# Rotary queries with fewer copies, input loads moved ahead, paged queries loaded early, and low halves moved to VectorE in a hybrid decoder layer

## The chip, the cores and the metric

The kernel runs on one core of a Trainium2 chip. The metric is the device time of one execution in microseconds (us). The core's engines each work through an instruction stream of their own, in order: TensorE (PE, matmuls and transposes; its weight loads are shown apart as PEld), VectorE (DVE), ScalarE (ACT), GpSimd (POOL) and SyncE (SP, which issues most DMAs). An instruction that waits holds up everything behind it on its engine.

## The reference

One inference step of a layer with two branches over the same input x: 1024 prompt tokens and 8 x 8 sampled tokens (1088 in all), width 1024. Cut to what matters here:

```python
xn = rmsnorm(x, w["norm_in"])
z = xn @ w["w_in"]
u_s, g_s, cq, ckv_raw, kr_raw, g_a, m_s, m_a = split_in(z)
y_s, h_last = s5_branch(u_s, ssm_h0, w)      # y = scan + d * u; zg = gelu(y)
                                             # out = zg * sigmoid(zg @ w_glu + b_glu)
y_s = (y_s * silu(g_s)) @ w["w_br_ssm"]
cq = rmsnorm(cq, w["mla_q_norm"])
q = einsum('blr,rhd->blhd', cq, w["mla_w_uq"])                 # 16 heads, 64 + 32
q_rope = apply_rope(q[..., 64:], cos, sin)   # x1, x2 = halves of 16:
                                             # [x1*cos - x2*sin, x1*sin + x2*cos]
...
o_lat = attend(q_lat, q_rope, ckv, k_rope)   # prompt: causal softmax;
                                             # sampled: 4096 paged tokens each, and themselves
y_a = (o * silu(g_a)) @ w["w_br_attn"]
merged = sigmoid(m_s) * y_s + sigmoid(m_a) * y_a
h = x + merged @ w["w_out"]                  # then rmsnorm(h, norm_final)
```

Everything is float32, and the new latents, rotary keys and scan states are outputs too.

## The kernel before

Each large product is computed from split operands. A float32 tensor is cast to a shorter format (the high half, `whi`, `z` by ScalarE in most places), the difference is taken as the low half (`wlo`, on VectorE or GpSimd), and three matmuls (high by high, high by low, low by high) add up in PSUM (`mm3`, L154). Activations stand transposed: eight rows of 128 channels by 1088 tokens, as `xT`, `z`, `aT`, `oT`, with a high and a low tile for each row. A product runs over chunks of 368, 368 and 352 tokens.

Streams of work are woven by generators that yield estimated costs, with an offset of priority for each stream. A scheduler with a timeline model then fixes the order on every engine, so the order of the code is only a hint. `behind` adds a dependency that this scheduler sees; it makes no semaphore wait.

The stages in the order of time: the norm and transposes of x and the scan input u, with the scan's setup (`s5_setup`) beside it, up to about 115 us; the scan with gate products as filling; latents; rotary queries and keys (484 to 541 us); query, key and value projections, with the gather of cached rotary keys, to 668; prompt attention with gate products and the gelu (`gy`, `gw`) to 975; then the gated unit on z, the ssm branch on a, and paged attention, to 1565; the attention branch on o; and the output product from 1682.

Places that the change touches:

- Input loads (L209): x is loaded in three groups of three tiles into six buffers, and each group's load is issued when its turn comes. The scan's setup loads c (L394, L395), b (L399, L400), d (L499) and the state (L505) on the same queue, SP.
- Rotary queries (L881 to L890): for each of 4 x 3 chunks, ScalarE copies the product out of PSUM, then copies it again in four blocks of 32 partitions, with the halves exchanged, into `qrot`. GpSimd multiplies the one by the cosines and the other by the sines, VectorE adds them, and the sum is split and stored to `qr_dram`.
- `load_split` (L109 to L112): loads a row of z, a or o over the place of an earlier tensor's row, casts it on ScalarE and takes the low half; GpSimd does so for rows 1, 3 and 5, VectorE for the others. The row of z stands where the row of `xT` stood, so its load waits for the last matmul on that row.
- The paged attention's queries `qs` (L1109, twelve loads), its mask (L1101) and its own new keys (L1114 to L1121) are set up when the paged attention begins. Its tiles are placed as they come.
- The final norm's weights `gf` are loaded at the start of the attention branch.

## Time and profile before

| | |
|---|---|
| Time, three runs | 1794.87, 1798.14, 1799.96 us; median 1798.14 |
| The profiled execution | 1795.67 us, of which the span is 1793.9 us |
| Mean granted clock of TensorE | 0.983 of full speed |
| Busy in the span | PE 96%, PEld 91%, DVE 61%, ACT 53%, POOL 37% |
| The chain that ended last, by engine | PE 73%, DMA 8%, DVE 6%, ACT 5%, issue 3%, POOL 3% |

TensorE is busy nearly all the time, so what other engines do counts only where TensorE waits for them. A row of a timeline gives the start, the busy time, engine, line, operation, output<-input and shapes, and in brackets the idle time just ahead of it with what ended that. The granted clock is a share of full speed; 0.50 is the lower of its two levels. Runs of the same form are joined in one row with a count (x3).

### The profile page before, as it was taken

The numbers are of one execution on the slowest core, as the hardware profiler recorded it, in microseconds if no ns is written. First come the engines' busy times: TensorE is split into PE (matmuls) and PEld (weight loads), VectorE is DVE, ScalarE is ACT, GpSimd is POOL, SyncE is SP. The second block draws the span as 40 slices with busy tenths as digits, with TensorE's granted clock in tenths as the row PEclk, the third lists the DMA queues.
The fourth block names the chain that finished last, engine by engine and source line by source line (L and its number), as shares of the span: only waits on it lengthen the run. The fifth ranks groups of instructions, "written<-read, shape, count | busy, mean of one in ns | idle before, by whom it ended". The sixth has DMA issues, their size and how long they took to land.

```text
span 1793.9 us, 32266 instructions
## 1 busy us (share of the span) xinstructions
PE 1715.3 (96%) x11434; PEld 1628.7 (91%) x11434; DVE 1102.7 (61%) x2552; ACT 944.5 (53%) x2287; POOL 671.6 (37%) x694
## 2 busy tenths in 40 slices
PE   6999999989989999999997999989999999999997
PEld 6999999989989998999996999879989999999997
DVE  6758898233354435878876887586656766554322
ACT  5236657623373434777765665266656666432222
POOL 1000000023462214656654555665545555232223
PEclk9999999999999999999998999999999999999999
DMA  8465345453559997667656453665555555375602
GB/s 214 110 150 151 110 127 132 121 148 110 154 167 308 321 321 204 151 163 187 172 142 202 128 149 86 213 222 173 182 173 165 184 176 181 103 238 162 180 1 100
DMA packets 263194, 299.59 MB, mean 167 GB/s; under 512 B 40273, under 2 KB 223289, under 8 KB 256761
## 3 DMA queue, kind: packets, MB, share of 16 engines
q1 hardware_dynamic: 252856, 240.89, 46.9%
q0 software_dynamic: 7872, 48.24, 8.0%
q10 hardware_dynamic: 2304, 8.39, 1.2%
q8 instruction: 91, 1.49, 0.3%
q14 instruction: 71, 0.57, 0.1%
HBM read 201.79 MB, written 95.66 MB: 166 GB/s over the span
## 4 chain that ended last, share of the span: by engine, by line
PE 73%; DMA 8%; DVE 6%; ACT 5%; issue 3%; POOL 3%; SPq 2%; POOLq 0%; ACTq 0%; DVEq 0%
PE mm L154 36%; PE sc L154 5%; PE acc L1155 5%; PE sc L1009 4%; PE tr L154 3%; PE tr L1045 3%; PE sc L1129 2%; PE sc L1218 2%; PE acc L1058 2%; PE acc L1059 2%; PE tr L1129 1%; PE tr L1218 1%; DMA ck<-cache_ckv,pidx 1%; DMA v_dram<-vt 1%; DMA kr_dram<-dks 1%
## 5 line engine op out<-in xcount | busy, mean ns | idle before, releaser
L154 PE MATMUL mm<-xT,whi 128*128 128x368 f32 (+1 forms) x1920 | 505.6, 337 | 3.3 <-ACT xT L237 1.5
L154 PEld LDWEIGHTS mm<-xT,whi 128*128 128x128 f32 x1920 | 342.1, 191 | 7.5 <-ACT xT L237 2.1
L154 PE MATMUL mm<-xT,wlo 128*128 128x368 f32 (+1 forms) x960 | 319.6, 334 | 0.0
L102 POOL TENSOR_TENSOR cl<-ck,ch 128x1024 fp32r<-128x1024 f32 x64 | 157.8, 2467 | 168.0 <-ACT ch L96 149.0
L154 PEld LDWEIGHTS mm<-xT,wlo 128*128 128x128 f32 x960 | 182.7, 190 | 1.0 <-issue 0.2
L102 DVE TENSOR_TENSOR pTl<-tr,pTh 128x256 fp32r<-128x256 f32 (+1 forms) x248 | 126.0, 511 | 39.6 <-ACT pTh L96 22.8
L96 ACT CAST pTh<-tr 128x256 fp32r<-128x256 f32 (+1 forms) x248 | 110.5, 449 | 73.3 <-PE tr L1045 58.0
L1009 PE MATMUL sc<-K,Q 128*128 128x384 f32 (+5 forms) x576 | 132.9, 349 | 8.9 <-ACT p L1021 8.9
L1191 POOL DMA_INDIRECT dkr<-cache_krope,pidx x32 | 34.1, 1067 | 267.0 <-DMA rt<-k_rope_tok 259.7
L1026 POOL TENSOR_SCALAR p<-p,sm 128x128 f32<-128x128 f32 (+7 forms) x128 | 97.4, 766 | 87.2 <-DVE sm L1025 41.6
L1021 ACT ACTIVATE p<-sc,sm 128x128 f32<-128x128 f32 (+2 forms) x192 | 110.8, 583 | 25.2 <-DVE sm L1016 14.9
L1045 PE MATMUL tr<-ident,p 128*128 128x128 f32 x576 | 113.0, 276 | 6.0 <-DVE sm L1016 3.0
L1009 PEld LDWEIGHTS sc<-K,Q 128*128 128x128 f32 x576 | 98.3, 191 | 16.9 <-ACT p L1021 11.9
L96 ACT CAST whi<-wraw 128x1024 fp32r<-128x1024 f32 (+1 forms) x76 | 73.4, 966 | 72.0 <-PE mm L154 61.1
L1013 DVE TENSOR_REDUCE sm<-sc 128x1 f32<-128x128 f32 (+3 forms) x192 | 103.1, 550 | 12.7 <-PE sc L1009 8.9
L154 PE MATMUL mm<-z,whi 128*128 128x368 f32 (+1 forms) x384 | 110.0, 349 | 0.0
L154 PE MATMUL mm<-aT,whi 128*128 128x368 f32 (+1 forms) x384 | 108.1, 340 | 0.3 <-ACT th L1392 0.3
L154 PE MATMUL mm<-oT,whi 128*128 128x368 f32 (+1 forms) x384 | 94.6, 328 | 2.9 <-DVE oT L112 1.6
L102 DVE TENSOR_TENSOR wlo<-wraw,whi 128x1024 fp32r<-128x1024 f32 (+1 forms) x54 | 63.4, 1174 | 51.4 <-ACT whi L96 50.1
L1045 PEld LDWEIGHTS tr<-ident,p 128*128 128x128 f32 x576 | 72.7, 142 | 12.7 <-DVE pTl L102 5.3
L1059 PE MATMUL acc<-pTl,Vt 128*128 128x256 f32 (+1 forms) x224 | 82.4, 368 | 0.3 <-DVE sm L1018 0.2
L96 ACT CAST ch<-ck 128x1024 fp32r<-128x1024 f32 x64 | 67.2, 1051 | 28.5 <-DMA ck<-cache_ckv,pidx 15.2
(472 smaller groups left out, 4553.3 us busy)
## 6 DMA issues: line engine op xcount, KB each, us to landing
wraw<-w_in SPq DMA_DIRECT2D x45, 512.0 KB
krT<-kr_dram SPq DMA_DIRECT2D x64, 192.0 KB
kr_dram<-krx SPq DMA_DIRECT2D x64, 128.0 KB
v_dram<-vt SPq DMA_DIRECT2D x32, 256.0 KB
Q<-qn_dram SPq DMA_DIRECT2D x32, 256.0 KB
...
```

Source lines behind the costliest of these rows:

```text
L96: nc.scalar.copy(hi, src)
L102: e.tensor_sub(lo, src, hi.bitcast(F32))
L154: i = nc.tensor.matmul(ps, row(s, k)[:, wsl], row(m, k)[(slice(None),) + xsl], start=start and k == j == 0, stop=stop and k == nk - 1 and ...
L1009: self.mark(nc.tensor.matmul(s[:, :w], qq[:, i * P:(i + 1) * P], kk[:, k0:k0 + w], start=j == 0, stop=j == 2), j == 0)
L1013: V.reduce_max(sm[:, x:x + 1], s[:, :w], axis=AX.X)
L1021: nc.scalar.activation(p[:, k0:k0 + w], s[:, :w], AF.Exp, bias=sm[:, 2:3], scale=SCALE, accum_out=sm[:, 3 + x:4 + x])
L1026: nc.gpsimd.tensor_scalar(p[:, :n], p[:, :n], sm[:, 5:6], 0.0, op0=ALU.mult, op1=ALU.add)
L1045: self.mark(nc.tensor.transpose(b[:, x * P:(x + 1) * P], ptl[x][:, k * P:(k + 1) * P], self.ident), x == s0)
L1059: nc.tensor.matmul(po[:, o0:], w, tl[:, o0:], start=False, stop=k == nk - 1)
L1129: i = nc.tensor.matmul(s, x[:, k], y[:, k], start=x is qlh and k == 0, stop=False)
L1155: self.mark(nc.tensor.matmul(o[:, :KV], t[:kp, i * P:(i + 1) * P], pv(i)[x], start=j == 0 and i == 0, stop=j == 2 and i == nt - 1), i == 0)
L1218: self.mark(nc.tensor.transpose(t[:, i * P:(i + 1) * P], ck[:, i, k * P:(k + 1) * P], self.ident), i == 0)
```

## The change

Five edits go together.

1. Rotary queries. The columns of the query weights are permuted on the host so that all first halves of a group of four heads stand in partitions 0 to 63 and all second halves in 64 to 127. The exchange is then two copies of 64 partitions instead of four of 32, the plain copy is gone, and VectorE multiplies by the cosines straight from PSUM. `qr_dram` has a new layout and is written in 16 pieces instead of 8.
2. Input loads. The second group of x is issued behind the first two weight loads, the third at the end of the first group's transposes, and the setup's loads of c, b, d and the state are ordered behind the third.
3. Paged queries. Their setup is called at the start of the prompt attention, into a pool that outlives it, with six loads instead of twelve. `dec_layout` fixes where the paged attention's tiles lie, and the split latents get three names of one buffer each.
4. Low halves of z, a and o are always taken by VectorE. The casts of rows of z and a are ordered behind the third next row of the product before (`ZD`).
5. The final norm's weights are loaded in the output stage.

```diff
-ZP = (1, 3, 5)
+ZD = 3
...
+    def load_split(self, t, k, src, urgent=0, behind=None):
...
-            nc.scalar.copy(hi, lo)
-            (nc.gpsimd if k % 8 in ZP else nc.vector).tensor_sub(t[1][k], lo, hi.bitcast(F32))
+            i = nc.scalar.copy(hi, lo)
+            if behind is not None:
+                self.behind(i, behind)
+            nc.vector.tensor_sub(t[1][k], lo, hi.bitcast(F32))
... (mm3: self.row_mm gets the last matmul of each row; stage_x:)
+        load(0)
+        for gi in range(3):
+            xs = loaded[gi]
...
+                load(1)
...
-                if k == KT - 1:
-                    self.x_last = self.x_last or i
                 yield 1.0
+            if gi == 0:
+                self.x_last = i
+                self.x_loads = load(2)
... (s5_setup: each of c, b, d and the state by later)
+        def later(out, src):
+            self.behind(nc.sync.dma_start(out, src), self.x_loads)
... (q_rope)
-            nc.scalar.copy(q, b[:, :m])
-            for c in (0, 64):
-                nc.scalar.copy(r[c:c + 32], b[c + 32:c + 64, :m])
-                nc.scalar.copy(r[c + 32:c + 64], b[c:c + 32, :m])
-            nc.gpsimd.tensor_mul(q, q, tabs[0][:, t0:t0 + m])
+            nc.scalar.copy(r[0:64], b[64:128, :m])
+            nc.scalar.copy(r[64:128], b[0:64, :m])
             nc.gpsimd.tensor_mul(r, r, tabs[1][:, t0:t0 + m])
+            nc.vector.tensor_mul(q, b[:, :m], tabs[0][:, t0:t0 + m])
             nc.vector.tensor_add(q, q, r)
             self.split(hi[:, t0:t0 + m], lo[:, t0:t0 + m], q, "act", "dve")
         for x, t in ((0, hi), (1, lo)):
-            nc.sync.dma_start(self.qr_dram[x, s], t.bitcast(F32))
+            for half in range(2):
+                nc.sync.dma_start(self.qr_dram[x, half, s * 64:s * 64 + 64], t[half * 64:half * 64 + 64].bitcast(F32))
... (dec_setup)
-            for x in range(2):
-                r0 = k * 32 + x * 16
-                dst = self.qs[r0:r0 + 16].rearrange("r (m e) c -> r m e c", e=2).bitcast(F32)
-                for e in range(2):
-                    nc.sync.dma_start(dst[:, :, e], qr[x, :, :, e])
+            for half in range(2):
+                r0 = k * 32 + half * 16
+                nc.sync.dma_start(self.qs[r0:r0 + 16].bitcast(F32), qr[half])
... (decode; dec_layout, not shown, allocates the tiles in a fixed order)
-                c = [sb.tile([P, 4, KV], F32R, name=n, bufs=3) for n in ("ch", "cl")]
+                c = [sb.tile([P, 4, KV], F32R, name=f"{n}{(b * 8 + g) % 3}", bufs=1) for n in ("ch", "cl")]
... (load_z; load_a alike)
-            self.load_split(z, k, self.z_dram[k * P:(k + 1) * P].rearrange("c t k -> c (t k)"), UZ)
+            self.load_split(z, k, self.z_dram[k * P:(k + 1) * P].rearrange("c t k -> c (t k)"), UZ,
+                            rows[min(k + ZD, KT - 1)])
... (stage_out)
+        gf = sb.tile([P, D], F32, name="gf", bufs=1)
+        nc.sync.dma_start(gf, a["norm_final"].partition_broadcast(P))
... (build)
                     self.attn_setup(kp, sb, ps)
+                    self.dec_setup(dcr, sb, ps)
                     yield from self.urgent(UP, self.prompt(sb, ps))
...
-                    self.dec_setup(sb, sb, ps)
+                    self.dec_layout(sb)
```

The order on the engines, at three places. SP at the start, behind the first two groups of x and two weight blocks; `xt` is x, `wraw` a block of weights, `ct`, `bt`, `dT` and `stt` are c, b, d and the state. Before:

```order
L395 DMA ct_549<-ssm_c_im 128x8x64
L399 DMA bt<-ssm_b_re 64x1024
L400 DMA bt_555<-ssm_b_re 64x1024
L399 DMA bt<-ssm_b_im 64x1024
L400 DMA bt_555<-ssm_b_im 64x1024
L118 DMA wraw<-w_in 128x8x128 x2
L499 DMA dT<-ssm_d 16x64x1
L118 DMA wraw<-w_in 128x8x128
L499 DMA dT<-ssm_d 16x64x1
L505 DMA stt<-state_ssm 128x256 x2
L209 DMA xt<-x_prompt 128x1024 x2
L209 DMA xt<-x_sample 64x1024
```

Now:

```order
L121 DMA wraw<-w_in 128x8x128 x3
L216 DMA xt<-x_prompt 128x1024 x2
L216 DMA xt<-x_sample 64x1024
L406 DMA ct<-ssm_c_re 128x8x64
L406 DMA ct_555<-ssm_c_re 128x8x64
L406 DMA ct<-ssm_c_im 128x8x64
L406 DMA ct_555<-ssm_c_im 128x8x64
L406 DMA bt<-ssm_b_re 64x1024
L406 DMA bt_561<-ssm_b_re 64x1024
L406 DMA bt<-ssm_b_im 64x1024
L406 DMA bt_561<-ssm_b_im 64x1024
L406 DMA dT<-ssm_d 16x64x1 x2
```

The last tiles of x moved ahead of c, b, d and the state; three weight blocks of this stretch stand ahead of them in both.

ScalarE where z begins. A `z_0` cast makes the high half of z's first row, `p` are exponentials of scores, `pTh` high halves of transposed probabilities, `oT` attention outputs. Before:

```order
L1021 ACTIVATE p_11379,sm<-sc,sm 128x384 x2
L96 CAST pTh<-tr 128x256
L1021 ACTIVATE p_11529,sm<-sc,sm 128x128
L96 CAST pTh<-tr 128x256
L111 CAST z_0_11852<-z_0_11853 128x1088
L1021 ACTIVATE p_11541,sm<-sc,sm 128x256
L96 CAST pTh<-tr 128x256 x2
L1021 ACTIVATE p_11558,sm<-sc,sm 128x448 x2
L96 CAST pTh<-tr 128x128
L111 CAST z_1_11854<-z_1_11855 128x1088
L1021 ACTIVATE p_11583,sm<-sc,sm 128x512
```

Now:

```order
L1038 ACTIVATE p_11372,sm<-sc,sm 128x384 x2
L1038 ACTIVATE p_11522,sm<-sc,sm 128x128
L96 CAST pTh<-tr 128x256 x2
L1038 ACTIVATE p_11534,sm<-sc,sm 128x256
L96 CAST pTh<-tr 128x256 x2
L1038 ACTIVATE p_11551,sm<-sc,sm 128x448 x2
L96 CAST pTh<-tr 128x128
L96 CAST pTh<-tr 128x512
L112 CAST z_0_11845<-z_0_11846 128x1088
L112 CAST z_1_11847<-z_1_11848 128x1088
L1080 COPY oT<-acc 64x512
L96 CAST pTh<-tr 128x512 x2
```

The cast of the first row moved behind the exponentials of 256 and 448 columns and four casts of probabilities, and the second row's cast stands right behind it.

SP and then ScalarE at the start of the prompt attention. `causal` is the mask, `gy` the scan's output for the gelu, `gw` the gelu's work tile, `K` keys, `dmask` and `qs` the paged attention's mask and queries. SP before:

```order
L1088 DMA Vt<-v_dram 128x2048
L964 DMA causal<-k_causal 128x128
L1365 DMA gy<-y_dram 128x156 x4
L786 DMA g_ga<-gst 128x1088
L118 DMA wraw<-w_in 128x8x128 x2
```

SP now:

```order
L1105 DMA Vt<-v_dram 128x2048
L981 DMA causal<-k_causal 128x128
L1118 DMA dmask<-k_self 128x512
L1124 DMA qs<-qr_dram 16x16x64 x6
L1401 DMA gy<-y_dram 128x156 x4
L804 DMA g_ga<-gst 128x1088
```

ScalarE before:

```order
L783 ACTIVATE gst<-mm 128x368 x2
L96 CAST K_7195<-sc 64x512
L1368 ACTIVATE gw<-gy 128x156
L96 CAST K_7197<-sc 64x512
L1372 ACTIVATE gw<-gw 128x156
L1021 ACTIVATE p_7253,sm<-sc,sm 128x128
L1021 ACTIVATE p_7302,sm<-sc,sm 128x256
```

ScalarE now:

```order
L801 ACTIVATE gst<-mm 128x368 x2
L96 CAST K_7170<-sc 64x512
L96 CAST K_7172<-sc 64x512
L1038 ACTIVATE p_7246,sm<-sc,sm 128x128
L1038 ACTIVATE p_7295,sm<-sc,sm 128x256
L96 CAST whi<-wraw 128x1024
L1404 ACTIVATE gw<-gy 128x156
L801 ACTIVATE gst<-mm 128x352
L1038 ACTIVATE p_7312,sm<-sc,sm 128x448 x2
L1408 ACTIVATE gw<-gw 128x156
```

On SP seven loads came in ahead of the gelu's. On ScalarE the gelu's first instruction moved behind both key casts, two exponentials and a weight cast.

## Rows read from the trace of the kernel before

**Rows 1.** The page's part 1: busy time of each engine, share, instructions.

```profile
PE 1715.3 (96%) x11434; PEld 1628.7 (91%) x11434; DVE 1102.7 (61%) x2552; ACT 944.5 (53%) x2287; POOL 671.6 (37%) x694
```

**Rows 2.** By stretch: us, PE, PEld, DVE, ACT, POOL busy, clock, DMA share, GB/s.

```profile
36.10:39.40 3.30, 0.03 (x1) 0.00 (x1) 1.61 (x6) 2.22 (x5) 0.55 (x1) 0.90 0.22 50
39.40:49.60 10.20, 8.99 (x35) 6.99 (x36) 8.14 (x36) 5.09 (x12) 1.15 (x2) 0.53 0.00 0
515.00:525.00 10.00, 4.14 (x24) 3.61 (x23) 4.97 (x9) 8.03 (x17) 4.17 (x5) 0.92 0.61 208
525.00:530.00 5.00, 5.00 (x18) 5.00 (x17) 3.81 (x6) 4.23 (x11) 3.65 (x5) 0.50 0.73 239
600.00:668.00 68.00, 68.00 (x437) 63.43 (x436) 29.05 (x60) 30.77 (x81) 11.62 (x12) 1.00 0.94 321
940.00:980.00 40.00, 29.86 (x163) 26.64 (x161) 26.93 (x62) 24.35 (x52) 17.41 (x14) 0.87 0.63 186
980.00:1000.00 20.00, 19.24 (x111) 17.80 (x112) 16.61 (x47) 10.70 (x31) 9.93 (x10) 0.91 0.67 174
1200.00:1220.00 20.00, 15.92 (x91) 13.72 (x90) 17.73 (x31) 11.97 (x23) 9.53 (x5) 0.91 0.64 198
```

**Rows 3.** Timeline of SP's queue at the start: start, us, issue.

```profile
21.71 3.85 SPq L499 DMA_DIRECT2D dT<-ssm_d  x1
...
31.31 0.85 SPq L209 DMA_DIRECT2D xt<-x_prompt  x2
```

**Rows 4.** By tile, qr and qrot, and line L784: duration ns min/median/max; waiters.

```profile
L881 ACT COPY qr<-sc x6: 452/466/467, 483.6 to 528.9; 128x368 f32<-128x368 f32 x4, 128x352 f32<-128x352 f32 x2
...
L883 ACT COPY qrot<-sc x12: 442/457/460, 484.1 to 530.4; 32x368 f32<-32x368 f32 x8, 32x352 f32<-32x352 f32 x4
...
L886 POOL TENSOR_TENSOR qrot<-qrot,tab x12: 934/978/995, 486.0 to 535.6; 128x368 f32<-128x368 f32 x8, 128x352 f32<-128x352 f32 x4
L887 DVE TENSOR_TENSOR qr<-qr,qrot x12: 514/538/2976, 487.1 to 537.6; 128x368 f32<-128x368 f32 x8, 128x352 f32<-128x352 f32 x4
...
524.35 0.66 PE L1201 MATMUL sc<-ident,dks 128*128 128x128 f32 x2 [4.16 <-ACT qrot L884]
...
L784 DVE SCALAR_TENSOR_TENSOR gst<-gst,mm x48: 502/527/539, 270.8 to 716.2; 128x368 f32<-128x368 f32 x32, 128x352 f32<-128x352 f32 x16
```

**Rows 5.** Timeline, SP, ScalarE, TensorE: loads of paged queries; start of prompt attention.

```profile
1140.03 12.67 SPq L1109 DMA_DIRECT2D qs<-qr_dram  x12
...
683.55 3.56 SPq L1365 DMA_DIRECT2D gy<-y_dram  x4
...
691.14 0.33 ACT L1368 ACTIVATE gw<-gy 128x156 f32<-128x156 f32 x1 [3.66 <-DMA gy<-y_dram]
...
693.59 1.07 PE L1009 MATMUL sc<-K,Q 128*128 128x448 f32 x3 [2.92 <-ACT p L1021]
```

**Rows 6.** Timeline of TensorE and VectorE at the start of paged attention.

```profile
1144.06 0.41 PE L1129 MATMUL tr<-ckS,dql 128*128 128x64 f32 x2 [3.17 <-DVE dql L1245]
...
1139.80 4.20 DVE L1245 TENSOR_TENSOR dql<-dql,dqh 128x256 fp32r<-128x256 f32 x1 [2.04 <-ACT dqh L1244]
```

**Rows 7.** Timeline of four engines in the z stage; last, z's waits by tile.

```profile
950.50 1.10 ACT L111 CAST z<-z 128x1088 fp32r<-128x1088 f32 x1 [7.11 <-DMA z<-z_dram]
...
952.12 1.65 PE L1009 MATMUL sc<-K,Q 128*128 128x512 f32 x3 [5.08 <-ACT p L1021]
...
980.76 0.62 PE L1045 MATMUL tr<-ident,p 128*128 128x128 f32 x2 [2.99 <-DVE sm L1016]
...
951.63 1.29 DVE L112 TENSOR_TENSOR z<-z,z 128x1088 fp32r<-128x1088 f32 x1 [5.14 <-ACT z L111]
...
976.04 3.31 DVE L112 TENSOR_TENSOR z<-z,z 128x1088 fp32r<-128x1088 f32 x1
...
975.82 2.38 POOL L102 TENSOR_TENSOR wlo<-wraw,whi 128x1024 fp32r<-128x1024 f32 x1 [1.10 <-PE sc L1009]
...
  DMA z<-z_dram: 10.2, 5
```

More of the change, by code (lines that the diff above doesn't have):

```diff
@@ L150, in mm3s @@
         n = 0
+        self.row_mm = []
         for k in range(nk):
@@ L159, in mm3s @@
                     n += 1
+            self.row_mm.append(i)
         self.last_mm = i
@@ L203, in stage_x, with load @@
         toks = tiles_of_tokens()
-        for gi in range(3):
+        loaded = []
+        def load(gi):
             xs = []
@@ L208, in stage_x @@
                 src = a["x_prompt"][0, t0:t0 + P, :] if t0 < SEQ else a["x_sample"].rearrange("b t d -> (b t) d")
-                nc.sync.dma_start(xt[:pt], src)
+                i = nc.sync.dma_start(xt[:pt], src)
                 xs.append((xt, t0, pt))
+            loaded.append(xs)
+            return i
+        load(0)
+        for gi in range(3):
+            xs = loaded[gi]
             if gi == 0:
@@ L393, in s5_setup @@
             src = a[nm].rearrange("(j g) c p -> (g c) j p", j=8)
-            nc.sync.dma_start(ct[:, :, x], src)
-            nc.sync.dma_start(ct2[:, :, 1 - x], src)
+            later(ct[:, :, x], src)
+            later(ct2[:, :, 1 - x], src)
         bt = sb.tile([G, 2, SP, GC], F32, name="bt", bufs=1)
@@ L398, in s5_setup @@
         for x, nm in ((0, "ssm_b_re"), (1, "ssm_b_im")):
-            nc.sync.dma_start(bt[:, x], a[nm])
-            nc.sync.dma_start(bt2[:, 1 - x], a[nm])
+            later(bt[:, x], a[nm])
+            later(bt2[:, 1 - x], a[nm])
         yield 5.0
@@ L498, in s5_setup @@
         for x in range(2):
-            nc.sync.dma_start(self.dT[x * GC:(x + 1) * GC], a["ssm_d"].rearrange("(g c) -> c g", c=GC))
+            later(self.dT[x * GC:(x + 1) * GC], a["ssm_d"].rearrange("(g c) -> c g", c=GC))
         self.h0 = sp.tile([P, NPR, 2, DB], F32, name="h0")
@@ L504, in s5_setup @@
             st = sb.tile([P, P, 2], F32, name="stt", bufs=2)
-            nc.sync.dma_start(st, hs[r * P:(r + 1) * P])
+            later(st, hs[r * P:(r + 1) * P])
             b = self.bank(ps)
@@ L990, in qkv_load @@
             self.first_load = self.first_load or i
-            qr = self.qr_dram[x, pr // 2].rearrange("(n x e f) c -> n e f x c", n=2, x=2, e=2)
-            self.nc.sync.dma_start(t[row:row + 32].bitcast(F32), qr[pr % 2, h, :, :, 0:SEQ])
+            qr = self.qr_dram[x].rearrange("a (h f) c -> h f a c", f=16)
+            self.nc.sync.dma_start(t[row:row + 32].bitcast(F32), qr[2 * pr + h, :, :, 0:SEQ])
             self.nc.sync.dma_start(self.KTs[h][x][r0:r0 + 64].bitcast(F32), self.kn_dram[x, rows])
@@ L1121, in dec_setup, with dec_layout, at @@
         nc.vector.tensor_copy(self.krs, b[:96, :NS])
+    def dec_layout(self, sb):
+        def at(name, n, bufs=1, dt=F32):
+            sb.tile([P, n], dt, name=name, bufs=bufs)
+        for name, n in (("pTh", 512), ("pTl", 512)):
+            at(name, n, dt=F32R)
+        at("dacc", KV, 2)
+        at("dst", 8, 2)
+        at("dnm", 4, 4)
+        at("dqh", 2 * P, 2, F32R)
+        at("pad0", 80)
+        sb.tile([96, P], F32R, name="dqr", bufs=2)
+        at("dql", 2 * P, 2, F32R)
+        sb.tile([96, 512], F32R, name="krT", bufs=KRB)
+        at("dp", 512, 2)
+        at("ch2", 4 * KV, dt=F32R)
+        at("pad1", 256)
+        at("ck", 8 * KV, 2)
     def dec_scores(self, s, q, ck, kr, n):
@@ L1377, in load_z @@
     def load_z(self, z):
+        rows = self.row_mm
         for k in range(KT):
-            self.load_split(z, k, self.z_dram[k * P:(k + 1) * P].rearrange("c t k -> c (t k)"), UZ)
+            self.load_split(z, k, self.z_dram[k * P:(k + 1) * P].rearrange("c t k -> c (t k)"), UZ,
+                            rows[min(k + ZD, KT - 1)])
             yield 0.0
@@ L1414, in load_a @@
     def load_a(self, aT):
+        rows = self.row_mm
         for k in range(KT):
-            self.load_split(aT, k, self.a_dram[k * P:(k + 1) * P], UZ)
+            self.load_split(aT, k, self.a_dram[k * P:(k + 1) * P], UZ, rows[min(k + ZD, KT - 1)])
     def stage_br_ssm(self, aT, raws, outs, sb, ps, goals):
```

20 lines of the change are left out of this document (9 added, 11 removed).

## The prediction

> **What bounds the kernel now.** I read the busy totals first, then tables by stretch where TensorE is not busy, then in those stretches what ends its waits. TensorE is busy 1715.3 of 1793.9 us [rows 1], so 79 us are idle, and the change can win only there and where the granted clock is down. The reader is to see four holes in [rows 2]. From 36.1 to 49.6 us TensorE is busy 0.03 + 8.99 us, the second part at a clock of 0.53, mostly the lower level of 1.2 GHz; at full clock (2.4 GHz) that is 8.99 x 0.53 = 4.8 us of work, so 8.7 of 13.5 us are lost. From 515 to 530 it is 4.14 x 0.92 + 5.00 x 0.50 = 6.3 us, so 8.7 of 15 are lost. From 940 to 1000 it is 29.86 x 0.87 + 19.24 x 0.91 = 43.5, so 16.5 of 60 are lost. From 1200 to 1220 it is 15.92 x 0.91 = 14.5, so 5.5 are lost.
>
> **Input loads.** The new SP order issues the third group of x right behind five weight loads; before, it stood behind the loads of c, b, d and the state. One d load alone held SP 3.85 us, and x was issued at 31.31 [rows 3]. After, it needs the first group's buffers and its turn in the queue. All of x (4.4 MB) and five weights of 0.5 MB at the 321 GB/s of the fullest stretch [rows 2] are 21 us, so I estimate a landing between 21 and 26, well ahead of 36. Late next is VectorE, where the scalings of the third group stand in one queue with the scan's setup, and the 1.2 us idle in the second part of the hole stay possible. The loads of c, b and d land later, and the setup's transposes stand some 50 matmuls further back on TensorE; the chain behind them has to move up as well for the gain to last, which is what the lower end is for. Gain between 0 and 8.7; I take 7.
>
> **Rotary queries.** Per chunk ScalarE does one copy of 0.466 and four of 0.457 us, and now two. A copy takes the same for 32 and for 128 rows [rows 4], so I take 0.457 for 64. Twelve chunks: 12 x (2.29 - 0.91) = 16.6 us less. GpSimd loses one product of 0.978 per chunk, 11.7 us. VectorE gains a product from PSUM; the trace does not show it. The nearest row is the gate's product from PSUM, 0.527 [rows 4], so 12 x 0.527 = 6.3 us. Its other end is the longest of the sums of queries, 2.98: 35.8 us. I take 0.527, since that row reads PSUM too. From PSUM to the sum the chain was five copies and two products (2.29 + 1.96); now two copies and one product (0.91 + 0.98): 2.4 us shorter per chunk. TensorE waited 4.16 us for a last copy [rows 4]. Gain 0 to 8.7, or a loss of up to 8 if the product took its other end in a stretch where VectorE is busy 3.81 of 5 [rows 2]; I take 6. Sixteen writes of half the rows replace eight: the same bytes, no term.
>
> **Paged queries.** Their twelve loads held SP 12.67 us at the start of the paged attention. Now six, and the mask, stand ahead of the first four gelu loads, which took 3.56 us of SP [rows 5]. Seven issues at the 0.89 of a gelu load are 6.2 us, at the 1.06 of an old query load 7.4. Who waits: ScalarE stood 3.66 us for the gelu input, a key cast behind it, and TensorE 2.92. In the new ScalarE order key casts and the first exponentials stand ahead of that instruction, and gate weights and the next exponentials behind it, so the lateness hits later. Between +2.9 and -7.4; I take -2. At the old place TensorE waited 3.17 us for the low half of the latent query, which took VectorE 4.20 [rows 6]. Neither its load nor its engine changes, only what stands around it: 0 to 3.2, I take 1.
>
> **Casts and low halves of z, a and o.** ScalarE stood 7.11 us at the cast of the first z row, waiting for its load, with exponentials behind it, and TensorE 5.08 for one of these [rows 7]. Now the exponentials and probability casts of that moment stand ahead of the cast. (The rule that puts them there orders the program and adds no wait.) VectorE gets three low halves more in z, 3 x 1.29 = 3.9 us at the time of one without GpSimd beside it. The 3.31 us one stood beside a weight half on GpSimd, with the maxima behind it that TensorE waited 2.99 for [rows 7]; weight halves stay on GpSimd, so some of this stays. The casts of rows 4 to 6 now stand together, and each waits for a load that SP issues only when a row of x is done: this landing is late next, for one or two waits of 2 us. Gain 0 to 16.5, or a loss down to 3 x 3.31 = 9.9; I take 11, the first wait with its clock and half of the rest. For a the edit is the same, in a stretch where VectorE is busy 17.73 of 20 us [rows 2]: three more low halves against GpSimd's going, -9.9 to +5.5; I take 1. For o, three more, with no cast moved: -3.9 to as much the other way, I take 0. The final norm's weights, one load ahead of nine on SP, cost an issue of some 0.43 us (two x loads took 0.85, [rows 3]) under the last matmuls of the stage: 0.
>
> **Sum.** 7 + 6 - 2 + 1 + 11 + 1 + 0 = 24 us off the profiled execution's 1795.67 (1793.9 of span, 1.8 around it), which is 1771.7. That execution is 2.5 below the median of 1798.14, so the forecast on the scale of the runs is 1774.
>
> **Rivals.** A: the z stage stays bound by its loads, since the order of casts can't bring a row of z before its row of x is done. Then 3 of the 11 us come, and the attention's start costs 5: 7 + 6 - 5 + 3 = 11, so 1787. For it: five casts waited for loads, 10.2 us in all [rows 7]. Against: the first is 7.11 of these.
> B: each closed hole also keeps the clock up, and nearly all goes: 8.7 + 8.7 + 16.5 + 5.5 - 2 = 37, so 1761. For it: the parts behind a hole at 0.53 and 0.50. Against: a new order on five engines brings waits of its own.
> C: no difference. What is won ahead of 541 us is given back in the stretch where the DMA engines are busy 0.94 and an earlier turn lands no earlier, and z wins 3 while a loses as much: 1798. Against: TensorE is busy all of 600 to 668 [rows 2], so the transfers do not yet end its waits there.
> D: slower. VectorE's low halves become the path. Nine move there, and beside GpSimd each costs up to 3.31: 29.8 us, the softmax's maxima queued behind them. With two thirds on the path (20), no gain left in z and a, and 7 + 6 - 2 + 1 = 12 from the rest, it ends 8 above: 1806. It decides from 12 us on the path. For it: 3.31 in [rows 7], 17.73 of 20 in [rows 2]. Against: 1.29 in [rows 7], and the change takes GpSimd's own low halves away from beside VectorE's.
>
> The pair of 1.29 and 3.31 [rows 7] is what D rests on. The Trainium skill, SBUF — State Buffer, Who interferes with whom, says that a VectorE instruction with two SBUF inputs contends with a GpSimd instruction that reads SBUF, and one with at most one SBUF input outside the 2-port modes does not. All low halves have two SBUF inputs, so the rule speaks against moving them. GpSimd was busy 27.3 of 60 us in the z stage [rows 2], about a third of the time without its three low halves; by the rule nine would cost 9 x (0.33 x 3.31 + 0.67 x 1.29) = 17.6 us, two thirds of which is 12, and D would land on no change, not on 1806. The trace agrees on these two rows, and on the product from PSUM (0.50 to 0.54 in 48 of 48, [rows 4]) by the other half of the rule.
>
> **How the numbers follow.** The forecast (15 to 30 us won) has 0.50, A 0.22, B 0.12, C 0.09, D 0.07. Its own range is 1768 to 1783. A measurement of this kernel can't tell less than 0.3% (5.4 us) from no change, 1792.7 to 1803.5. Faster: forecast, B and nearly all of A, 0.82; same: C and A's slow tail, 0.10; slower: D and some of C, 0.08. For 8 in 10 I reach from 1757 (a little beyond B) to 1796 (A, and part of C).
>
> **What would show it.** In the new profile: TensorE busy and the clock at 1.0 from 36 to 50 us; 24 copies of rotary queries of 0.46 us and twelve products near 0.53; no wait over 2 us in the rotary stage; no ScalarE wait of 7 us for z, and over 54 of 60 us busy there; the gelu's first instruction waiting as long as before with no exponential behind it. Wrong: low halves at 3 us on VectorE with TensorE waiting for maxima, ScalarE waits of over 3 us each for rows 4 to 6 of z, over 5 us idle at the attention's start, or idle time between 541 and 668.

## The result and the profile after

The changed kernel takes 1777.1 us, the median of 5 runs (1773.56 to 1777.57), against 1798.14 of before (5 runs). The ratio is 0.9881, 95% interval 0.9863 to 0.9898: 21 us faster. The forecast was 1774. The profiled execution took 1777.57 us, which is 18.1 us under that of before; its span is 1775.7. A second job with the same file gave 0.9867 (0.9845 to 0.9889), 23 to 24 us.

The page's part 1 of the kernel after: busy time, share, instructions. It answers to [rows 1].

```profile
PE 1705.0 (96%) x11434; PEld 1622.0 (91%) x11434; DVE 1105.7 (62%) x2573; ACT 928.4 (52%) x2251; POOL 631.9 (36%) x673
```

TensorE executes the same 11434 matmuls in 10.3 us less busy time (its mean granted clock is 0.987, and was 0.983), and is idle 70.7 instead of 78.6 us. ScalarE loses 16.1 us and GpSimd 39.7, VectorE gains 3.0. What matters is where TensorE runs earlier. Both kernels have the same number of matmuls, so the start of the n-th can be set against the start of the n-th, each from its trace's first instruction. This table is worked out from the two traces so; the columns are the number n, when it starts in before, and how much earlier it starts after, called the lead below (us).

```
    n    before    earlier    what lies ahead of it
  600     117       4.3       input loads
 2600     386       2.9
 3600     557       7.3       rotary queries
 4400     683       8.3
 4800     752       6.9       start of the prompt attention
 6200     991      14.5       first half of z
 7200    1157      10.0       rest of z, start of the paged attention
 7600    1228      14.4       a
 8600    1381      16.4       paged attention
 9800    1559      15.3
10200    1620      18.2       o; stays so to the end
```

The second job's trace of the same file gives 5.2, 3.5, 7.0, 7.9, 6.9, 13.4, 7.9, 12.8, 16.4, 16.3 and 18.5, so a single entry is good to some 2 us.

The kernel after by stretch, columns as in [rows 2].

```profile
24.00:27.50 3.50, 0.97 (x10) 0.73 (x8) 2.56 (x12) 2.70 (x8) 1.13 (x2) 1.00 1.16 236
27.50:34.00 6.50, 5.95 (x28) 5.54 (x29) 5.76 (x18) 4.41 (x9) 0.54 (x1) 0.74 1.05 207
34.00:44.00 10.00, 10.00 (x59) 8.29 (x58) 7.31 (x30) 4.52 (x9) 0.00 (x0) 1.00 0.16 29
490.00:500.00 10.00, 9.89 (x60) 9.47 (x59) 9.11 (x14) 5.61 (x14) 7.28 (x8) 1.00 0.67 185
500.00:510.00 10.00, 8.71 (x53) 8.11 (x52) 9.79 (x15) 7.00 (x16) 5.54 (x7) 1.00 0.72 202
510.00:520.00 10.00, 6.41 (x32) 6.14 (x31) 8.08 (x14) 4.88 (x11) 5.17 (x5) 0.86 0.92 255
940.00:960.00 20.00, 16.96 (x109) 15.64 (x107) 17.58 (x43) 16.07 (x34) 5.50 (x6) 1.00 0.75 226
960.00:980.00 20.00, 16.58 (x80) 15.07 (x81) 16.40 (x35) 9.71 (x25) 9.50 (x8) 0.74 0.78 215
980.00:1000.00 20.00, 18.84 (x123) 17.87 (x122) 16.92 (x47) 13.29 (x36) 12.54 (x11) 1.00 0.52 130
1200.00:1220.00 20.00, 17.91 (x122) 15.72 (x121) 15.31 (x35) 12.56 (x28) 9.08 (x5) 1.00 0.59 211
```

Busy time by clock, as the prediction did it: the old hole at 36 to 50 us is gone (10.00 of 10 at 1.00), but a new one of 4.6 us stands at 24 to 34 (3.50 - 0.97, and 6.50 - 5.95 x 0.74). The rotary stage still loses 10 + 10 + 10 - 9.89 - 8.71 - 6.41 x 0.86 = 5.9 us of the 8.7, z 60 - 16.96 - 16.58 x 0.74 - 18.84 = 11.9 of the 16.5, and a 2.1 of the 5.5. Such stretches hold somewhat different work, since the kernel after runs 3 to 18 us ahead: of the whole rotary stage, 484 to 530 before and 478 to 520 after, 9.7 and 6.1 us are lost.

**Start.** The kernel after, ScalarE, then TensorE, then SP's loads:

```profile
23.09 1.06 ACT L235 ACTIVATE xjunk<-xt 128x1024 f32<-128x1024 f32 x1 [3.02 <-DVE s_dt L349]
25.04 1.06 ACT L235 ACTIVATE xjunk<-xt 128x1024 f32<-128x1024 f32 x1 [0.80 <-DVE s_dt L364]
26.80 1.06 ACT L251 ACTIVATE xT<-sc,nrm_in 128x384 fp32r<-128x384 f32 x2
...
27.44 0.60 PE L158 MATMUL mm<-xT,whi 128*128 128x368 f32 x2 [2.53 <-ACT xT L251]
...
16.57 1.87 SPq L216 DMA_DIRECT2D xt<-x_prompt  x2
```

The third group of x is issued at 16.57 us instead of 31.31 [rows 3]. Its squares now stand in ScalarE's stream ahead of the second group's last casts to `xT`, and ScalarE stands there 3.02 + 0.80 us with TensorE behind it. The profile names `s_dt`, a tile of the scan that a square does not read; the landing of x, at the 6.4 us that its loads take here, falls at the same time.

**Rotary queries.** The kernel after by tile, columns as in [rows 4]; last, who waited for the sums.

```profile
L899 ACT COPY qrot<-sc x6: 448/462/466, 477.9 to 508.8; 64x368 f32<-64x368 f32 x4, 64x352 f32<-64x352 f32 x2
L901 POOL TENSOR_TENSOR qrot<-qrot,tab x12: 938/980/1260, 478.9 to 512.4; 128x368 f32<-128x368 f32 x8, 128x352 f32<-128x352 f32 x4
L902 DVE TENSOR_TENSOR qr<-sc,tab x6: 512/527/542, 479.1 to 510.4; 128x368 f32<-128x368 f32 x4, 128x352 f32<-128x352 f32 x2
L903 DVE TENSOR_TENSOR qr<-qr,qrot x12: 511/532/1900, 479.9 to 514.9; 128x368 f32<-128x368 f32 x8, 128x352 f32<-128x352 f32 x4
L102 DVE TENSOR_TENSOR ql<-qr,qh x12: 516/624/3256, 481.0 to 516.9; 128x368 fp32r<-128x368 f32 x8, 128x352 fp32r<-128x352 f32 x4
...
  DVE qr L903: 13.2, 8
```

A copy of 64 partitions takes 0.462 us, and the product from PSUM 0.51 to 0.54 in each. The sums still reach 1.90 and the low halves 3.26, and ScalarE waits 13.2 us for sums. TensorE's longest wait there is now for VectorE:

```profile
517.05 0.88 PE L158 MATMUL mm<-xT,whi 128*128 128x368 f32 x2 [3.59 <-DVE gst L802]
```

**Prompt attention's start.** The kernel after, SP, VectorE, TensorE:

```profile
673.94 0.34 SPq L981 DMA_DIRECT2D causal<-k_causal  x1
...
676.80 6.33 SPq L1124 DMA_DIRECT2D qs<-qr_dram  x6
...
683.37 0.50 DVE L1029 TENSOR_TENSOR sc<-sc,causal 128x128 f32<-128x128 f32 x2 [4.24 <-DMA causal<-k_causal]
...
686.05 1.49 PE L1026 MATMUL sc<-K,Q 128*128 128x448 f32 x3 [1.79 <-ACT p L1038]
```

VectorE waits 4.24 us for the causal mask, whose load was issued at 673.94, 9.4 us before the wait ends. TensorE waits 1.63 us for a piece of the paged attention's own new keys, whose work stands behind that on VectorE, and then the 1.79. The gelu loads behind the six query loads end no wait of TensorE.

**z, a and o.** The kernel after in z, TensorE, VectorE and GpSimd; then the low halves of z, a and o by tile, and z's wait for its loads:

```profile
948.72 0.98 PE L1026 MATMUL sc<-K,Q 128*128 128x512 f32 x3 [1.97 <-ACT p L1038]
...
965.32 0.66 PE L1062 MATMUL tr<-ident,p 128*128 128x128 f32 x2 [2.12 <-DVE pTl L102]
...
961.18 3.40 DVE L115 TENSOR_TENSOR z<-z,z 128x1088 fp32r<-128x1088 f32 x1
...
960.97 2.46 POOL L102 TENSOR_TENSOR wlo<-wraw,whi 128x1024 fp32r<-128x1024 f32 x1 [2.43 <-ACT whi L96]
...
L115 DVE TENSOR_TENSOR z<-z,z x8: 1274/1294/3396, 944.3 to 966.4; 128x1088 fp32r<-128x1088 f32 x8
...
L115 DVE TENSOR_TENSOR aT<-aT,aT x8: 1275/1293/2164, 1181.2 to 1208.5; 128x1088 fp32r<-128x1088 f32 x8
...
L115 DVE TENSOR_TENSOR oT<-oT,oT x8: 1221/1224/1226, 1557.6 to 1569.1; 128x1024 fp32r<-128x1024 f32 x8
...
  DMA z<-z_dram: 1.5, 1
```

The same low halves by tile in the kernel before, where five were VectorE's and three GpSimd's (2.39 to 2.61 us each):

```profile
L112 DVE TENSOR_TENSOR z<-z,z x5: 1292/2058/3314, 951.6 to 982.0; 128x1088 fp32r<-128x1088 f32 x5
...
L112 DVE TENSOR_TENSOR aT<-aT,aT x5: 1275/1672/3028, 1182.8 to 1217.6; 128x1088 fp32r<-128x1088 f32 x5
...
L112 DVE TENSOR_TENSOR oT<-oT,oT x5: 1211/1224/2775, 1573.6 to 1587.4; 128x1024 fp32r<-128x1024 f32 x5
```

The median of VectorE's falls from 2.06 to 1.29 us in z and from 1.67 to 1.29 in a, and the longest in o from 2.78 to 1.23. In z that is in part the new order: in the kernel after with three of eight on GpSimd again (below), the median of z is 1.36:

```profile
L113 DVE TENSOR_TENSOR z<-z,z x5: 1293/1364/2374, 942.2 to 968.2; 128x1088 fp32r<-128x1088 f32 x5
```

ScalarE's waits for rows of z fall from 10.2 us in five [rows 7] to 1.5 in one. The one low half of 3.40 us runs beside the weight half of 2.46 us on GpSimd, and TensorE then waits 2.12 us for a `pTl` queued behind it.

**Paged attention's start**, TensorE, is as before [rows 6], where it waited 3.17:

```profile
1133.43 0.64 PE L1165 MATMUL tr<-ckS,dql 128*128 128x64 f32 x2 [3.13 <-DVE dql L1281]
```

### The profile page after: what moved, and what is told of

The parts are those of the page before. It is cut to its first block, busy times and chain, and to the rows that moved or that the text cites. A ratio compares the mean times of both kernels' runs of the same rounds, so it can differ in the third digit from the quotient of the medians.

```text
span 1775.7 us, 32225 instructions
## 1 busy us (share of the span) xinstructions
PE 1705.0 (96%) x11434; PEld 1622.0 (91%) x11434; DVE 1105.7 (62%) x2573; ACT 928.4 (52%) x2251; POOL 631.9 (36%) x673
## 4 chain that ended last, share of the span: by engine, by line
PE 76%; DMA 8%; DVE 5%; issue 3%; ACT 3%; POOL 2%; SPq 1%; POOLq 0%; ACTq 0%; DVEq 0%
PE mm L158 37%; PE sc L158 6%; PE sc L1026 5%; PE acc L1191 4%; PE tr L158 3%; PE tr L1062 3%; DMA ck<-cache_ckv,pidx 2%; PE acc L1075 2%; PE acc L1076 2%; PE sc L1165 2%; PE sc L1254 2%; DMA wraw<-w_in 1%; PE tr L1254 1%; PE tr L1165 1%; DMA kr_dram<-dks 1%
## 5 line engine op out<-in xcount | busy, mean ns | idle before, releaser
L1038 ACT ACTIVATE p<-sc,sm 128x128 f32<-128x128 f32 (+2 forms) x192 | 110.7, 584 | 21.7 <-DVE sm L1033 11.9
L1030 DVE TENSOR_REDUCE sm<-sc 128x1 f32<-128x128 f32 (+2 forms) x192 | 104.2, 551 | 11.4 <-PE sc L1026 8.2
L1026 PEld LDWEIGHTS sc<-K,Q 128*128 128x128 f32 x576 | 99.6, 192 | 11.5 <-ACT p L1038 6.5
```

What stands on the lines that cost most here:

```text
L1026: self.mark(nc.tensor.matmul(s[:, :w], qq[:, i * P:(i + 1) * P], kk[:, k0:k0 + w], start=j == 0, stop=j == 2), j == 0)
L1030: V.reduce_max(sm[:, x:x + 1], s[:, :w], axis=AX.X)
L1038: nc.scalar.activation(p[:, k0:k0 + w], s[:, :w], AF.Exp, bias=sm[:, 2:3], scale=SCALE, accum_out=sm[:, 3 + x:4 + x])
```

## The experiments

All ratios are of the kernel before on the same chip, with 95% intervals. "Undone" and "alone" are kernels made from the one after.

### One part undone

Rotary stage as before, on the new layout:

```diff
-            nc.scalar.copy(r[0:64], b[64:128, :m])
-            nc.scalar.copy(r[64:128], b[0:64, :m])
-            nc.gpsimd.tensor_mul(r, r, tabs[1][:, t0:t0 + m])
-            nc.vector.tensor_mul(q, b[:, :m], tabs[0][:, t0:t0 + m])
+            nc.scalar.copy(q, b[:, :m])
+            for c in (0, 32):
+                nc.scalar.copy(r[c:c + 32], b[c + 64:c + 96, :m])
+                nc.scalar.copy(r[c + 64:c + 96], b[c:c + 32, :m])
+            nc.gpsimd.tensor_mul(q, q, tabs[0][:, t0:t0 + m])
+            nc.gpsimd.tensor_mul(r, r, tabs[1][:, t0:t0 + m])
```

> The changed kernel, but the rotary queries on the engines as before: one whole copy and four copies of 32 partitions on ScalarE, both products on GpSimd (the new order of weights and of the stored queries stays). Theory 1, from the trace of the changed kernel: the rotary stage only wins 2 to 4 us of TensorE, because the wait for a last copy (4.16 us) has turned into one for a gate's product on VectorE (3.59). Then this kernel is at 1779 to 1781, against 1777.1 for the whole change. Rival (the prediction's term): the edit is worth 6 us, and this kernel is at 1783. ScalarE copies of 32 partitions take 0.46 us again and TensorE waits over 5 us in the rotary stage by either.

Measured: 1783.76 us, 0.9931 (0.9904 to 0.9959). TensorE of this kernel:

```profile
519.83 0.45 PE L1239 MATMUL sc<-ident,dks 128*128 128x128 f32 x1 [4.17 <-ACT qrot L902]
```

The 4.16 us wait of [rows 4] is back as 4.17, and the lead of 5.0 us at n 2600 is -0.6 at n 3800. By the ratios, the kernel without the shorter chain is 9 to 11.5 us slower than the one after: more than the first theory's 2 to 4, and more than the rival's 6.

Input loads in the old order:

```diff
-        load(0)
         for gi in range(3):
+            load(gi)
...
-                load(1)
...
-                self.x_loads = load(2)
...
-            self.behind(nc.sync.dma_start(out, src), self.x_loads)
+            nc.sync.dma_start(out, src)
```

> The changed kernel, but x and the scan's setup are loaded in the order of before. Theory 1: the new load order wins only 4.2 us, since a new hole of 2.53 us with 3.4 us at the low clock stands at 25 to 32 us; this kernel is at 1781 and has the hole of 3.3 us at 36 us again. Rival: the lead is worth more later, since the scan's setup starts behind it, so 7 us, 1784; or it is given back before the attention, so that this kernel is at 1777.

Measured: 1784.76 us, 0.991 (0.9884 to 0.9936). The low clock of 10.2 us at 39 is back, and the lead at n 600 is 0.2 instead of 4.3. By the ratios, 5 to 8 us are lost: nearer the rival's 7 than the 4.2 of the first theory.

Paged queries set up at the paged attention's start, without `dec_layout`:

```diff
-                c = [sb.tile([P, 4, KV], F32R, name=f"{n}{(b * 8 + g) % 3}", bufs=1) for n in ("ch", "cl")]
+                c = [sb.tile([P, 4, KV], F32R, name=n, bufs=3) for n in ("ch", "cl")]
...
-                    self.dec_setup(dcr, sb, ps)
...
-                    self.dec_layout(sb)
+                    self.dec_setup(sb, sb, ps)
```

> The changed kernel, but the paged queries, the mask and the new keys are set up at the start of the paged attention (six loads, not twelve), its tiles placed as they come. Theory 1: where they are now they cost the prompt attention's start 1.4 us, and at the old place they would cost about as much; the wait for the low half of the latent query (3.13 us) is there in both. So 1776 to 1779, no difference that can be measured. Rival: SP held by these loads at the paged start makes TensorE wait, and this kernel is 3 us or more slower, 1780 or over.

Measured: 1778.23 us, 0.9897 (0.9857 to 0.9937), span 1773.6. No difference from the kernel after can be measured, as the first theory had it.

Low halves on GpSimd for rows 1, 3 and 5, and casts not ordered:

```diff
-            if behind is not None:
-                self.behind(i, behind)
-            nc.vector.tensor_sub(t[1][k], lo, hi.bitcast(F32))
+            (nc.gpsimd if k % 8 in (1, 3, 5) else nc.vector).tensor_sub(t[1][k], lo, hi.bitcast(F32))
```

> The changed kernel, but casts and low halves of z, a and o as before: three of eight low halves on GpSimd, no order behind the product before. Theory 1: z wins 7 us, a 4 and o 3, and 3 to 4 of these are given back, so this kernel is 10 to 11 us slower, 1787 to 1788, and ScalarE waits about 7 us at the first cast of z again. Rival: what z wins is lost in the rest of the prompt attention, and only 4 us are left, 1781.

Measured: 1783.15 us, 0.9915 (0.9889 to 0.9942), 6 to 9 us slower than the kernel after by the ratios, between the two theories; the intervals overlap a little. Its profiled execution, 1777.45, was one of its faster ones (1776.25 to 1786.09), and its span of 1775.7 is that of the kernel after. ScalarE at the first row of z here:

```profile
941.06 1.10 ACT L112 CAST z<-z 128x1088 fp32r<-128x1088 f32 x1 [3.59 <-DMA z<-z_dram]
```

It waits 3.59 us, not the 7.11 of [rows 7], though the rule on casts is out. The planner makes a new order from the other edits, and half of that hole went by this alone. So the trace of before is not the right base for this term. From 940 to 1000 us this kernel loses 8 of TensorE's 60 us (busy time by clock, as above), less than the 11.9 with the edit in place.

### One part alone, and the kernel after again

The unaltered kernel, for the scatter between jobs:

```diff
 (no edit)
```

> The changed kernel itself, unaltered, beside the three that follow, so that they are compared on one chip. 0.988 of the kernel before, as in the first result; its profile shows the holes of the changed kernel at the same places within 2 us.

Measured: 1772.85 us, 0.9867 (0.9845 to 0.9889).

Low halves alone, rotary stage alone, and loads alone are made of the edits above, three of them undone in each:

```diff
 s2: rotary stage, loads and paged queries as above
 s3: loads, paged queries and low halves as above
 s4: rotary stage, paged queries and low halves as above
```

> Only the casts and low halves of z, a and o are changed (and the new order of stored rotary queries and the late load of the final norm's weights, which move no work on the engines that wait); loads, rotary copies and paged queries are as before. Theory 1 (the prediction): each edit closes the hole at its own place; the wait of 7.11 us at z's first cast goes and this kernel wins 7 us in the z stage and keeps 4 of them or more, 1791 or less, ratio 0.996 or less. Theory 2, from undoing this edit, which cost the profiled execution nothing (1775.7 us of span with and without it): the z hole goes with the order that the planner happens to find, and this edit alone wins nothing in the end, 1796 to 1800, ratio 0.998 to 1.001.

Measured: 1790.45 us, 0.9962 (0.9947 to 0.9978). The total is that of the first theory, but not the place: from 940 to 1000 us this kernel still loses 14 of TensorE's 60 us (16.5 in before), and its lead is -6.8 us at n 7200 and 4.6 at the end.

> Only the rotary queries are changed (with their new order in memory, six loads of paged queries at the old place, and the late load of the final norm's weights). Theory 1 (the prediction): 6 us, 1792, ratio 0.997, won at the rotary stage and nowhere else; the z stage has its wait of 7.11 us. Theory 2, from undoing this edit, which cost 10 us, 9 of them between 440 and 560 us: 8 to 10 us, 1789, ratio 0.995 or less.

Measured: 1790.91 us, 0.997 (0.9955 to 0.9985).

> Only the load order of x and the setup is changed (with the new order of stored queries and the late load of the final norm's weights). Theory 1 (the prediction): 7 us, 1791. Theory 2, from the trace: 4.2 us at the start, ahead by 4 us to the end, 1794, ratio 0.998. Rival: it is given back in the rotary stage or the z stage, 1798.

Measured: 1790.11 us, 0.9968 (0.9952 to 0.9985). ScalarE in the last one, behind the rotary stage:

```profile
546.31 0.62 ACT L96 CAST wuvh<-wuvr 128x512 fp32r<-128x512 f32 x1 [3.95 <-DMA wuvr<-mla_w_uv]
...
555.09 0.37 ACT L96 CAST vt<-tr 128x256 fp32r<-128x256 f32 x1 [4.46 <-DMA v_dram<-vt]
```

Alone the parts are worth 6.8 (low halves), 5.4 (rotary) and 5.8 us (loads), in sum 18.0 of the 21 to 24 of all together; each interval allows about 2.8 us either way, so the rest need not be an effect of their company. The profiled execution of the loads alone (1797.17) was the slowest of its twelve: its lead of 5.1 us at n 600 is 0.5 at n 3800, while ScalarE waits 3.95 us for a weight load and 4.46 for a store of v (1.02 and 2.12 at the same two casts in before). That is rival C's mechanism, in one execution; in the median the loads keep 5.8.

### What is left in the new holes

Third group's squares behind the second group's last cast, and the causal mask's load issued early:

```diff
-                nc.scalar.activation(junk[:pt], xt[:pt], AF.Square, accum_out=st[:pt, 0:1])
+                i = nc.scalar.activation(junk[:pt], xt[:pt], AF.Square, accum_out=st[:pt, 0:1])
+                if gi == 2:
+                    self.behind(i, cast)
...
-        nc.sync.dma_start(self.causal, a["k_causal"])
+        with self.tc.high_priority(offset=US):
+            nc.sync.dma_start(self.causal, a["k_causal"])
```

> The changed kernel with two orders altered, far apart in the program. At the start the third group's sums of squares are ordered behind the second group's casts on ScalarE. At the prompt attention's start the mask's load (causal) gets priority, ahead of the loads of queries, keys and values. Theory 1: the hole at 25 to 27 us stands there because ScalarE takes the sums, which wait for x to land, ahead of the casts that TensorE needs, so it goes (2.5 us, and the clock behind it); the hole at 684 us stands there because VectorE waits 4.24 us for the mask with a key's low half and the new keys' last piece behind it, so TensorE's 1.63 and 1.79 go, and the clock behind it: together 5 to 7 us, 0.983 to 0.985 of the kernel before. Rival: the first hole is VectorE's queue (setup of the scan between the scalings) and the second the late gelu loads behind the six query loads; then both holes stay within 1 us and the ratio at 0.987.

Measured: 1774.16 us, 0.9863 (0.9838 to 0.9889): no difference from the kernel after that can be measured. Its profiled execution, 1779.35, was one of its slower ones (1770.2 to 1779.6). By stretch, and then TensorE's and ScalarE's waits:

```profile
24.00:27.50 3.50, 3.50 (x28) 3.18 (x27) 1.89 (x7) 2.48 (x6) 0.00 (x0) 1.00 1.09 201
27.50:34.00 6.50, 6.50 (x43) 6.44 (x42) 6.20 (x23) 5.40 (x10) 0.75 (x2) 1.00 1.05 231
...
538.28 0.37 ACT L96 CAST vt<-tr 128x256 fp32r<-128x256 f32 x1 [6.13 <-DMA v_dram<-vt]
538.98 0.32 PE L942 MATMUL sc<-qn,wukT 64*128 64x64 f32 x1 [3.44 <-ACT wukT L936]
...
695.00 0.96 PE L1031 MATMUL sc<-K,Q 128*128 128x512 f32 x3 [1.29 <-ACT p L1043]
...
718.14 0.33 ACT L1409 ACTIVATE gw<-gy 128x156 f32<-128x156 f32 x1 [5.44 <-DMA gy<-y_dram]
...
719.68 0.96 PE L1031 MATMUL sc<-K,Q 128*128 128x512 f32 x3 [2.81 <-ACT p L1043]
```

Both holes close: TensorE is busy 10.00 of 10 us from 24 to 34, and no wait over 1.3 us is left between 668 and 719. But both gains are given back. The lead over the kernel after, 3.4 us at n 600, is 0.7 at n 3600: ScalarE waits 6.13 us at 538 for a store of v (3.65 in the kernel after), and TensorE 3.44 behind it. The lead over before rises from 9.0 to 12.6 us between n 4400 and 4500, at the attention's start, and is 6.7 at n 4700: ScalarE waits 5.44 us at 718 for a gelu load with exponentials behind it, and TensorE 2.81 for one of these.

Casts of rows 4 to 7 of z left free, instead of all behind the product's last row:

```diff
-                            rows[min(k + ZD, KT - 1)])
+                            rows[k + ZD] if k < 4 else None)
```

> The changed kernel, but only the casts of rows 0 to 3 of z are ordered behind the product before; those of rows 4 to 7 come where the planner puts them, one by one between exponentials. Theory 1: the z stage lost 2.38 and 2.12 us and 10.2 us at the low clock because the casts of rows 4 to 6 stood in a row (3.1 us) ahead of a gate's activation and the probability casts on ScalarE, and their low halves in a row on VectorE; spread, 4 to 6 us come back there. 0.984 to 0.986 of the kernel before. Rival: loads of z decide, and casts put earlier wait for them with exponentials behind, so that the stage loses 2 us or more: 0.989.

Measured: 1780.5 us, 0.99 (0.9875 to 0.9925). ScalarE and TensorE:

```profile
955.05 1.10 ACT L112 CAST z<-z 128x1088 fp32r<-128x1088 f32 x1 [2.15 <-DMA z<-z_dram]
...
956.88 1.17 PE L1026 MATMUL sc<-K,Q 128*128 128x384 f32 x3 [3.10 <-ACT p L1038]
```

A free cast waits 2.15 us for its load with exponentials behind it, and TensorE 3.10. By the theory that the crowded casts are what is left in z, 4 to 6 us should have come back, and none did. Loads of z hold the free casts, as the rival had it, and the ratio is near its 0.989, though the interval overlaps that of the kernel after.

The sine product on VectorE too:

```diff
-            nc.gpsimd.tensor_mul(r, r, tabs[1][:, t0:t0 + m])
+            nc.vector.tensor_mul(r, r, tabs[1][:, t0:t0 + m])
```

> The changed kernel with the sine product of the rotary queries on VectorE too, none on GpSimd. Theory 1: sums and low halves of the rotary queries (two inputs in SBUF) were stretched to 1.3 to 3.3 us by GpSimd's products beside them, and VectorE's last wait of 3.6 us for a gate's product came from that; with no product on GpSimd they take 0.53 each and the wait falls under 2 us: 2 us faster. Rival: VectorE's queue of twelve times three operations is the path whoever runs beside it; twelve products more (6.4 us) make TensorE's wait there longer, 2 to 5 us slower.

Measured: 1766.93 us (1766.09 to 1770.61), 0.983 (0.9806 to 0.9855). Its tile rows and stretches:

```profile
L901 DVE TENSOR_TENSOR qrot<-qrot,tab x12: 512/532/545, 480.5 to 507.9; 128x368 f32<-128x368 f32 x8, 128x352 f32<-128x352 f32 x4
L903 DVE TENSOR_TENSOR qr<-qr,qrot x12: 515/531/543, 481.5 to 510.5; 128x368 f32<-128x368 f32 x8, 128x352 f32<-128x352 f32 x4
L102 DVE TENSOR_TENSOR ql<-qr,qh x12: 514/532/690, 482.6 to 511.8; 128x368 fp32r<-128x368 f32 x8, 128x352 fp32r<-128x352 f32 x4
...
  DVE qr L903: 4.3, 5
```

```profile
490.00:500.00 10.00, 10.00 (x63) 9.97 (x62) 10.00 (x24) 7.67 (x18) 1.74 (x3) 1.00 0.77 224
500.00:510.00 10.00, 10.00 (x64) 9.98 (x63) 9.28 (x20) 7.85 (x17) 2.25 (x3) 1.00 0.84 237
510.00:520.00 10.00, 10.00 (x63) 9.97 (x62) 3.81 (x8) 1.90 (x5) 1.63 (x2) 1.00 0.99 321
```

VectorE was the busier engine (9.79 of 10 us at 500), got twelve products more, and was done sooner: the sums fall from up to 1.90 to 0.54, the low halves from up to 3.26 to 0.69, and TensorE is busy all of 490 to 520. From its first rotary product to the last low half, VectorE takes 38.4 us in the kernel after, 31.1 of them busy (36.2 and 31.9 in the second job's trace); here, with the twelve products that are new to it, it takes 31.9, 28.5 of them busy. So twelve products at 0.98 on GpSimd had cost more in VectorE's slower instructions than twelve at 0.53 on VectorE itself. VectorE's waits for GpSimd's product go as well, 3.2 us in the one trace and 0.4 in the other, and what each of the two is worth was not separated. The lead over the kernel after is 6.8 us at n 3600 and 8.0 at n 4800, where the first theory expected 2 us. The ratio's interval lies below that of the kernel after and overlaps that of the second job. This is the lowest median time of all.

All three edits together:

```diff
 x4: the squares and the mask of x1, and the product of x3
```

> The changed kernel with all three of the last alterations that closed a hole: sums of squares behind the casts at the start, the mask's load first, and no rotary product on GpSimd. Theory 1: with the rotary stage no longer waiting, the 3 us won at the start and the 2 us at the prompt attention's start are kept; 4 to 5 us below the kernel with the rotary product moved alone, 0.980 to 0.981 of the kernel before. Rival: what is won at the start is given back where ScalarE waits for a store of v in the stretch that is full of transfers (6.13 us at 538 us when only the start was mended, 3.65 in the changed kernel); then no faster than 0.983.

Measured: 1769.58 us, 0.982 (0.9797 to 0.9844): the same as with the product alone. The 3.1 us that it leads by at n 600 are 1.4 at n 4800 and -2.8 at the end, so what the start wins is given back, as the rival had it, if not only at the store of v: the early mask's gain (the lead over the product alone goes from 0.7 at n 4400 to 4.8 at n 4500) is 1.4 at n 4700, and 2.2 us go in the first half of z and 3.9 at a (n 7200 to 7600). By which waits these last two go was not settled.

## Why the prediction was right, point by point

**Sum.** Right in sign and in size: 21 us against 24, inside the likeliest case's own range. The terms were less right than the sum, and that they add up so well is in part luck: z, the largest, did not give what it was priced at, and a, the paged attention and o, priced at 2 together, made up for much of it.

**Input loads, 7.** The mechanism was right and the size a little high: 4.3 us in the profile, 5.8 alone. The step that failed is what comes late next. It named VectorE's scalings of the third group; it was ScalarE's squares of it, which stand ahead of the second group's casts and wait for x. The squares experiment shows this, since the hole closes when they stand behind. The estimate that x lands between 21 and 26 us held.

**Rotary queries, 6.** 5.4 us alone, 9 to 11.5 in company. Copies at 0.46 and a product at 0.527 came out as priced. "No wait over 2 us in the rotary stage" was wrong, with 3.59 left. The prediction asked what the new product on VectorE costs and not what the product left on GpSimd costs VectorE's sums, though a sum of 2.98 stood in [rows 4]. That was some 7 us more, shown by the sine product on VectorE (6.8 at n 3600); a lesser part of it can be VectorE's waits for GpSimd's product.

**Paged queries, -2 and 1.** The start of the prompt attention cost 1.4 us (1.0 in the second trace), but not by the reason given: VectorE waits for the causal mask, not ScalarE for the gelu loads. The early mask shows that, since the waits of 1.63 and 1.79 us are gone with it. The reason given is the brake that comes next: with the mask early, ScalarE waits 5.44 us for a gelu load. The 1 at the paged attention's start did not come (3.13 against 3.17), and the early place of the queries can be left out without a measurable loss.

**Casts and low halves, 11 + 1 + 0.** The sum of this term was too high, 6.8 us alone and 6 to 9 in company, and its place was wrong. In the kernel after the lead rises 7.6 us in the first half of z, but 4.5 of that are gone behind the second half and the paged attention's start, and the edit is not shown to have won the rest. Over all of z (n 4800 to 7200) the traces of the nine kernels and repeats that have this edit as it is gain 2.5 us in the mean (-2.3 to 6.3), and those of the three without it 1.9 (-1.8 to 6.8). So the step that failed is the one from the 7.11 us to a gain: a new order alone made that wait 3.59, and with the edit alone TensorE's 60 us there still lose 14. What the edit does at the place is that ScalarE's waits for rows of z are 1.5 us in one (3.4 in two with the edit alone), against 5.9 in five without it. "Over 54 of 60 us busy" was missed with 52.4, at a clock of 0.74 in a third of it. The wait for loads that was priced at "one or two waits of 2 us" came as 1.50 on ScalarE and 1.97 on TensorE.

The gain is behind z. From n 7200 to 10200, which is a, the paged attention and o, the nine traces gain 8.8 us in the mean (5.4 to 11.4) and the three 1.6 (0.1 to 3.4). a was under-sized: 4.4 us between n 7200 and 7600, where TensorE is now busy 17.91 of 20 at a clock of 1.00 against 15.92 at 0.91 [rows 2]; in the mean it is 4.2 with the edit and 1.9 without. o, priced at 0, has 2.9 between n 9800 and 10200 (2.2 to 3.4 in the nine traces, -0.7 to 0.7 in the three). No cast of o is ordered, so this part is the low halves' alone: VectorE's longest is 1.23 us, where it was 2.78.

**Rivals.** A was right on z, in brake and in size: with the casts spread, loads of z end ScalarE's and TensorE's waits, and all of z gave the kernel after 3.1 us (6.9 at n 4800, 10.0 at n 7200; 1.0 in the second trace), where A had 3. It did not decide, as the attention's start cost 1.4 and not 5, the rotary stage kept its gain, and a, the paged attention and o gave more than either case had. B did not come: holes remain in each stage. C's mechanism shows in the edits made on top of this change (the squares' lead is given back at 538), and not, in the median, for the loads themselves. D did not come: VectorE's low halves did not become longer with GpSimd's gone (medians of 1.22 to 1.29 us); the longest left are one of 3.40 in z, beside a weight half, and one of 2.16 in a. By the Trainium skill's rule (SBUF — State Buffer, Who interferes with whom) the same contention holds for any VectorE instruction with two SBUF inputs beside a GpSimd instruction that reads SBUF. The rotary sums agree with it, up to 1.90 us with GpSimd's product beside them and up to 0.54 without. So does the product from PSUM, 0.51 to 0.54 in all twelve, by the rule's other half.

**What stays open.** How much of the gain at a is the low halves' and how much the order of the casts: there the two were always undone together. By which waits the lead won at the start goes in z and at a. The late load of the final norm's weights, priced at 0, and the new layout of `qr_dram` are in every kernel made here, so neither was tested. An earlier start of the latent query's low half, for the 3.13 us at the paged attention, was not tried.
